# Hybrid decoder trunk on one core: activations and gated heads turned by VectorE and SBUF-to-SBUF transfers instead of TensorE

## The chip, the core and the metric

The kernel runs on one core of one Trainium2 chip. The metric is the device time of one execution in microseconds (us). The kernel before takes 2820.26 us, the median of three runs from 2818.15 to 2820.35 us.

A core has five instruction streams that the text calls by the profile's names: PE is TensorE (matrix products), DVE is VectorE, ACT is ScalarE, POOL is GpSimd, and SP is SyncE, which here does nothing but issue transfers. Each works through its own list in order. SBUF is the on-chip memory of 128 partitions; PSUM holds the products of PE.

## The reference, cut to what matters

The trunk has two layers, each a token mixer and a feed-forward network (FFN), over 256 tokens of width 2048 in float32.

```python
def swiglu(h, w_gate, w_up, w_down):            # D_FF = 5632
    return (jax.nn.silu(h @ w_gate) * (h @ w_up)) @ w_down

def gdn_mixer(h, w_in, conv_w, a_log, dt_bias, head_norm, w_out):   # layer 0, 32 value heads of 128
    ...
    o = gated_delta_rule_chunked(q, k, v, beta, g).astype(h.dtype)
    o = rmsnorm(o, head_norm) * jax.nn.silu(z.reshape(B, S, GDN_V_HEADS, GDN_HEAD_V))
    return o.reshape(B, S, GDN_VAL_DIM) @ w_out

def hgrn2_mixer(h, w_in, lower_bound, head_norm, w_out):            # layer 1, 16 heads of 128
    ...
    o = rmsnorm(o, head_norm) * jax.nn.silu(gate)
    return o.reshape(B, S, HGRN_VAL_DIM) @ w_out

for layer in range(DEPTH):
    h = h + mixer(rmsnorm(h, ...), ...)
    h = h + swiglu(rmsnorm(h, ffn_norm[layer]), ...)
return rmsnorm(h, final_norm)
```

Two products matter here: the one with `w_down`, whose left side is the gated activation, and the one with `w_out`, whose left side is the gated and normed head output. Both left sides are computed with tokens on the partitions, and PE needs them with features on the partitions. So they must be transposed, 256 tokens by some hundred features at a time.

## The kernel before, in words

**Stages.** In order of time: the GDN mixer (about 0 to 820 us), FFN 0 (to about 1550), the HGRN mixer (to about 2080), FFN 1 (to the end). Every stage is a list of *groups*. A group streams its weights from HBM in *halves* of 128 by 1024 floats (512 KB) and adds up its products in a PSUM tile `main`. Float32 products are made of three fast ones: each weight half `raw` is split into a rounded part `wh` (ACT) and the rest `wl` (DVE), each left side into `xt_h`/`xt_l`, `ht_h`/`ht_l` (`hth`, `htl` in the profile) or `ot_h`/`ot_l`, and PE multiplies high by high, high by low and low by high. A half in the FFN, or of a `w_out` product, is 12 PE products of 128 by 512.

**The weight stream.** `stream` issues one load of `raw` on SP for each half (945 in all) into four buffers, and `wh` and `wl` have four buffers each. A load waits until DVE has read the buffer it overwrites; `wh` waits until PE has used the one it overwrites.

**The order.** The program records all operations, and `plan` sorts them for each engine by an event-driven model: operations have costs (`price`, `COST`), transfers have an issue cost and a landing time, and the operation with the earliest due time goes first among those that are ready. The streamed `main` products keep their order on PE, and all other PE work ("aux") is fitted between them. What `plan` has settled is fixed; on the chip each engine only waits for what it needs.

**The work around the change.** `gate_up` in `ffn` ends a group of 8 halves with `h1` (128 tokens by two token halves by 256 features; `h` in the profile): ACT makes `sg`, DVE multiplies. Every second group, PE transposes the two `h1` tiles with eight 128x128 products by `ident` into two PSUM tiles, and ACT and DVE write `hth` and `htl` from there. There are 22 groups in each FFN, in two parts of 12 and 10, and after each part four `down` groups use `hth` and `htl`. `head_out` does the same for four heads at a time: `zs` (128 by 2 by 512) holds the gated heads, PE transposes it with eight products, and ACT and DVE write `ot_h` and `ot_l`. GDN calls it 8 times (head groups 0 to 7) and HGRN 4 times. `out_proj` then multiplies two head groups by a slice of `w_out`, in four groups of four halves; in each group the first two halves use the first head group, the last two the second.

`GDN_ORDER` sets the order of GDN's groups (k, v and z are the input products of a head group, o is an `out_proj` of two):

```python
GDN_ORDER = (
    "k0 k1 k2 k3 v0 v1 z0 z1 v2 z2 k4 k5 v3 z3 v4 k6 o0 k7 v5 z4 z5 o1 v6 v7 z6 z7 o2 o3"
)
```

So head group 7 is the last to be finished, while o2 streams, and o3 needs it in its third half. In `gdn_inverse`, four transfers on SP bring `wide` for a chain of small DVE operations.

Of the kernel before, what the change touches and what calls it, by code (L numbers as in the profile page):

```python
# [147 lines left out]
class Recorder:  # L148
# [158 lines left out]
    def plan(self):  # L307
# [70 lines left out]
        while len(order) < len(ops):  # L378
# [127 lines left out]
class Trunk:  # L506
# [116 lines left out]
    def mm_rows(self, ps, i, wh, wl, n_chunks, operand, halves=range(2)):  # L623

        for k in range(2):
            xh, xl = operand(2 * i + k)
            cols = slice(k * 512, (k + 1) * 512)
            for tt in halves:
                tok = slice(tt * P, (tt + 1) * P)
                out = ps[tt] if isinstance(ps, tuple) else ps[:, tt, :]  # L630
                for m, (s, w) in enumerate(((xh, wh), (xh, wl), (xl, wh))):
                    self.nc.tensor.matmul(
                        out, s[:, tok], w[:, cols],
                        start=(i == 0 and k == 0 and m == 0),
                        stop=(i == 2 * n_chunks - 1 and k == 1 and m == 2),
                    )
# [14 lines left out]
    def mm_cols(self, ps, i, wh, wl, n_k, n_f, n_chunks):  # L651

        for k in range(n_k):
            kt = i * n_k + k
            xh, xl = self.operand(kt)
            for f in range(n_f):
# [58 lines left out]
    def make_xt(self, cg, norm):  # L715
# [11 lines left out]
        for pair, ps in enumerate(two):  # L727
            for k in range(2):
# [36 lines left out]
    def ffn(self, j, after):  # L765
        nc, a = self.nc, self.a
        hts, h1s = {}, {}

        def gate_up(gi):
            def end(ps):  # L770
                h1 = self.tile(self.pool, [P, 2, T], "h1", bufs=4)
                for tt in range(2):
# [10 lines left out]
                pair = hts[gi // 2] = tuple(  # L783
                    self.tile(self.pool, [P, 4, T], f"ht{x}", F32R, bufs=max(FF_PARTS) // 2) for x in "hl"
                )
                two = self.aux(), self.aux()
                nc.together(*two)
                for of, tr in enumerate(two):
                    for k in range(2):
                        for tt in range(2):  # L790
# [4 lines left out]
                for of, tr in enumerate(two):  # L795
                    ht, lt = (t[:, 2 * of : 2 * of + 2, :].rearrange("p a t -> p (a t)") for t in pair)
                    nc.scalar.activation(ht, tr, AF.Copy)
                    nc.vector.tensor_tensor(out=lt, in0=tr, in1=ht.bitcast(F32), op=ALU.subtract)

# [377 lines left out]

    def head_out(self, o, zs, scale, norm):

# [31 lines left out]
        for tt in range(2):  # L1211
            for h in range(4):
# [4 lines left out]
                )  # L1217
        oh, ol = (t([P, 4, T], f"ot_{x}", dt=F32R, bufs=3) for x in "hl")
        two = self.aux(), self.aux()
        nc.together(*two)  # L1220
        for b, tr in enumerate(two):
            for h in range(2):
                for tt in range(2):
# [4 lines left out]
        for b, tr in enumerate(two):  # L1228
            s = slice(2 * b, 2 * b + 2)
            self.split_scaled(  # L1230
                oh[:, s, :].rearrange("p h t -> p (h t)"), ol[:, s, :].rearrange("p h t -> p (h t)"),
                tr, norm,
            )
        return oh, ol

    def gdn_o(self, hg, st):
# [85 lines left out]
    def out_proj(self, name, p, states, last, after):  # L1322
# [210 lines left out]
    def hgrn_o(self, g, st):  # L1533
# [4 lines left out]
        for tok in range(2):  # L1538
            for h in range(4):
# [201 lines left out]
```

## Time and profile before

| | |
|---|---|
| median of three runs | 2820.26 us |
| span of the profiled execution, first to last instruction | 2817.3 us |
| instructions | 39806 |
| PE busy | 2800.8 us, 15198 matmuls |
| DVE busy | 1744.5 us |
| ACT busy | 1423.1 us |
| POOL busy | 254.0 us |
| moved by the 16 DMA engines | 580.46 MB, 206 GB/s over the span |

The profile gives no separate time for the profiled execution; its span is 2817.3 us, and the median of the runs is 2.96 us above it.

How to read it: a row of operations gives line, engine, operation, output and inputs by the program's names, shapes, count, busy time and the mean duration of one in ns, then the idle time of its engine just before. All operations are issued by one helper, so every row has line 489, and tile names tell them apart. Matmul durations overlap: consecutive products start every 0.227 us although each lasts 0.39 us.

### The profile page before, as it was taken

The page shows a single profiled execution, that of the slowest core. Times are in us where ns is not written, and L with a number is a line of the kernel's source. Part 1 is how long each engine was busy: PE and PEld are TensorE (multiplying, and loading weights), DVE is VectorE, ACT ScalarE, POOL GpSimd, SP SyncE. Part 2 cuts the span into 40 slices and gives each one's busy share as a digit, 9 for nine tenths or more (in the row PEclk, how much of TensorE's full clock was granted, in tenths as well). Part 3 has the DMA queues.
Part 4 walks back from the last instruction along what each step waited for, and adds up shares of the span by engine and source line. Part 5 has one row for each costly group of instructions (what it writes and reads, how often), then busy time and mean ns, then how long its engine had stood idle before and what let it go on. Part 6 is the DMA issues. An engine that isn't in the chain of part 4 may idle for free.

```text
span 2817.3 us, 39806 instructions
## 1 busy us (share of the span) xinstructions
PE 2800.8 (99%) x15198; PEld 2392.1 (85%) x15198; DVE 1744.5 (62%) x2511; ACT 1423.1 (51%) x1988; POOL 254.0 (9%) x370
## 2 busy tenths in 40 slices
PE   9999999999999999999999999999999999999998
PEld 9988888888888888888888999999888888888887
DVE  6787888777765555445455677678555455445554
ACT  6646666564554444344445555556454444344443
POOL 1213222222110000000000100000110000000000
PEclk9999999999999999999999999999999999999999
DMA  7686668778786655666557645545785556765564
GB/s 254 197 275 206 211 221 260 219 216 263 228 252 193 188 193 187 223 223 189 192 189 227 203 149 164 168 149 163 228 265 189 192 188 207 224 204 193 187 199 160
DMA packets 162672, 580.46 MB, mean 206 GB/s; under 512 B 20138, under 2 KB 21306, under 8 KB 162352
## 3 DMA queue, kind: packets, MB, share of 16 engines
q1 hardware_dynamic: 138912, 503.15, 55.6%
q0 software_dynamic: 23280, 73.91, 8.5%
q8 instruction: 119, 1.95, 0.3%
q10 hardware_dynamic: 288, 0.85, 0.1%
q14 instruction: 73, 0.60, 0.1%
HBM read 550.52 MB, written 27.31 MB: 205 GB/s over the span
## 4 chain that ended last, share of the span: by engine, by line
PE 99%; ACT 0%; DVE 0%; issue 0%; POOLq 0%; POOL 0%; ACTq 0%
PE main L489 91%; PE aux L489 8%; ACT dec L489 0%; DVE wl L489 0%; ACT wh L489 0%; DVE u L489 0%; ACT xt_h L489 0%; DVE utmp L489 0%; DVE pre L489 0%; ACT y L489 0%; POOLq L1737 0%; ACT junk L489 0%; DVE xl L489 0%; DVE ot_l L489 0%; POOL coll L489 0%
## 5 line engine op out<-in xcount | busy, mean ns | idle before, releaser
L489 DVE TENSOR_TENSOR wl<-raw,wh 128x1024 fp32r<-128x1024 f32 x945 | 1161.5, 1230 | 974.7 <-ACT wh L489 972.1
L489 ACT ACTIVATE wh<-raw 128x1024 fp32r<-128x1024 f32 x945 | 1000.7, 1060 | 1270.9 <-PE main L489 1221.7
L489 PE MATMUL main<-wh,xt_h 128*128 128x512 f32 x2176 | 850.5, 391 | 0.6 <-ACT wh L489 0.6
L489 PE MATMUL main<-wh,xt_l 128*128 128x512 f32 x2176 | 849.9, 391 | 0.0
L489 PE MATMUL main<-wl,xt_h 128*128 128x512 f32 x2176 | 848.7, 390 | 0.9 <-DVE wl L489 0.9
L489 PEld LDWEIGHTS main<-wl,xt_h 128*128 128x128 f32 x2176 | 408.6, 188 | 84.7 <-DVE wl L489 1.3
L489 PEld LDWEIGHTS main<-wh,xt_h 128*128 128x128 f32 x2176 | 408.6, 188 | 84.0 <-ACT wh L489 1.0
L489 PEld LDWEIGHTS main<-wh,xt_l 128*128 128x128 f32 x2176 | 408.6, 188 | 83.7
L489 PE MATMUL main<-xt_h,wl 128*128 128x256 f32 (+1 forms) x1040 | 292.3, 281 | 1.5 <-DVE wl L489 1.5
L489 PE MATMUL main<-xt_l,wh 128*128 128x256 f32 (+1 forms) x1040 | 291.8, 281 | 0.3 <-DVE xt_l L489 0.3
L489 PE MATMUL main<-xt_h,wh 128*128 128x256 f32 (+1 forms) x1040 | 290.1, 279 | 0.0
L489 PE MATMUL main<-wh,hth 128*128 128x512 f32 x664 | 258.7, 390 | 0.0
L489 PE MATMUL main<-wh,htl 128*128 128x512 f32 x664 | 258.6, 389 | 0.0
L489 PE MATMUL main<-wl,hth 128*128 128x512 f32 x664 | 258.3, 389 | 0.0
L489 PEld LDWEIGHTS main<-xt_h,wh 128*128 128x128 f32 (+1 forms) x1040 | 195.6, 188 | 0.3
L489 PEld LDWEIGHTS main<-xt_h,wl 128*128 128x128 f32 (+1 forms) x1040 | 193.8, 186 | 2.0 <-DVE wl L489 1.9
L489 PEld LDWEIGHTS main<-xt_l,wh 128*128 128x128 f32 (+1 forms) x1040 | 193.8, 186 | 0.9 <-DVE xt_l L489 0.5
L489 PE MATMUL main<-wh,ot_l 128*128 128x512 f32 x384 | 151.2, 394 | 0.6 <-DVE ot_l L489 0.6
L489 PE MATMUL main<-wh,ot_h 128*128 128x512 f32 x384 | 150.6, 392 | 0.9 <-ACT ot_h L489 0.9
L489 PE MATMUL main<-wl,ot_h 128*128 128x512 f32 x384 | 150.3, 391 | 0.0
L489 PEld LDWEIGHTS main<-wh,htl 128*128 128x128 f32 x664 | 124.6, 188 | 25.9
L489 PEld LDWEIGHTS main<-wl,hth 128*128 128x128 f32 x664 | 124.6, 188 | 25.7
(207 smaller groups left out, 2226.5 us busy)
## 6 DMA issues: line engine op xcount, KB each, us to landing
raw<-in_ffn_gu SPq DMA_DIRECT2D x352, 512.0 KB, 3.8
raw<-in_ffn_d SPq DMA_DIRECT2D x176, 512.0 KB, 4.5
raw<-in_hgrn_in SPq DMA_DIRECT2D x128, 512.0 KB, 3.7
raw<-in_gdn_kq SPq DMA_DIRECT2D x64, 512.0 KB, 4.9
raw<-in_gdn_v SPq DMA_DIRECT2D x64, 512.0 KB, 4.6
raw<-in_gdn_z SPq DMA_DIRECT2D x64, 512.0 KB, 4.9
raw<-in_gdn_out SPq DMA_DIRECT2D x64, 512.0 KB, 4.9
x_home<-x POOLq DMA_DIRECT2D x36, 512.0 KB, 5.1
```

Of the source, the lines that this page charges most:

```text
L489: getattr(getattr(tc.nc, op.eng), op.method)(*args, **kw)
```

## The change

Both transposes leave PE. A new function `turn` has DVE turn each 32 by 32 block of the tile in place of its position (one instruction), and then sixteen transfers on SP move the blocks, one for each pair of a source quarter and a target quarter of the partitions, back into the tile that was turned. Each transfer moves 32 partitions by 128 floats (16 KB) for `h1`, or by 256 floats (32 KB) for `zs`. After them the columns are in an order that the rearranged views undo. `h1` is turned after every group and no longer in pairs. ACT and DVE write the high and low parts from SBUF and no longer from PSUM; `ot_l` takes four DVE instructions of 128 by 256 in place of two of 128 by 512. The tiles that hold the parts are laid out by token half first, so `mm_rows` takes its left side by token half. Where `zs` is turned, the blocks go through the buffer of `r` (GDN) or `v` (HGRN), which is no longer needed then. In `plan`, SP is taken to be busy for 0.1 us instead of 0.45 with a transfer smaller than a fifth of a weight half. The transposes of the residual stream (`make_xt`) stay on PE.

```diff
-            clock[e] = at + max(0.45, LOAD_EVERY * op.share) if e == "sync" else done
+            clock[e] = at + max(0.1 if op.share < 0.2 else 0.45, LOAD_EVERY * op.share) if e == "sync" else done
...
+    def turn(self, x, blocks):
+        nc = self.nc
+        width = x.shape[1] // 4
+        nc.vector.transpose(
+            blocks.rearrange("p (c a j) -> p a c j", c=4, j=32), x.rearrange("p (a c i) -> p a c i", c=4, i=32)
+        )
+        for q in range(4):
+            for c in range(4):
+                nc.sync.dma_start(
+                    x[32 * c : 32 * c + 32, q * width : (q + 1) * width],
+                    blocks[32 * q : 32 * q + 32, c * width : (c + 1) * width],
+                )
+        return x.rearrange("p (q a j) -> p a q j", q=4, j=32)
...
     def ffn(self, j, after):
-                h1s[gi] = h1
-                if gi % 2 == 0:
-                    return
-                two = self.aux(), self.aux()
...
-                            nc.tensor.transpose(
-                                tr[:, k * T + tt * P : k * T + (tt + 1) * P],
-                                h1s[gi - 1 + of][:, tt, k * P : (k + 1) * P], self.ident,
-                            )
...
+                blocks = self.tile(self.pool, [P, 512], "blocks", bufs=2)
+                turned = self.turn(h1.rearrange("p t c -> p (t c)"), blocks)
...
+                nc.scalar.activation(as_turned(ht), turned, AF.Copy)
+                nc.vector.tensor_tensor(
+                    out=as_turned(lt), in0=turned, in1=as_turned(ht.bitcast(F32)), op=ALU.subtract
+                )
...
-    def head_out(self, o, zs, scale, norm):
+    def head_out(self, o, zs, scale, norm, blocks):
...
-                    nc.tensor.transpose(
-                        tr[:, h * T + tt * P : h * T + (tt + 1) * P],
-                        zs[:, tt, (2 * b + h) * P : (2 * b + h + 1) * P], self.ident,
-                    )
...
+        turned = self.turn(zs.rearrange("p t c -> p (t c)"), blocks)
+        nc.scalar.activation(as_turned(oh), turned, AF.Copy, scale=norm)
+        for q in range(4):
+            nc.vector.scalar_tensor_tensor(
+                out=as_turned(ol)[:, :, q], in0=turned[:, :, q], scalar=norm,
+                in1=as_turned(oh.bitcast(F32))[:, :, q], op0=ALU.mult, op1=ALU.subtract,
+            )
```

How the planned order moves is shown at four places.

ACT in an FFN, before: one pair of groups, from `sg` of the second group.

```order
L489 ACTIVATE sg_9108<-main_8948,rstd_61 128x256
L489 ACTIVATE sg_9114<-main_8948,rstd_61 128x256
L489 ACTIVATE wh_9122<-raw_9065 128x1024
L489 ACTIVATE wh_9143<-raw_9083 128x1024
L489 ACTIVATE hth_8761<-aux_9140 128x512
L489 ACTIVATE hth_8761<-aux_9149 128x512
L489 ACTIVATE wh_9175<-raw_9102 128x1024
```

ACT in an FFN, now, from `sg` of any group:

```order
L489 ACTIVATE sg_9889<-main_9706,rstd_61 128x256
L489 ACTIVATE sg_9895<-main_9706,rstd_61 128x256
L489 ACTIVATE wh_9904<-raw_9846 128x1024
L489 ACTIVATE wh_9934<-raw_9864 128x1024
L489 ACTIVATE wh_9959<-raw_9883 128x1024
L489 ACTIVATE wh_9977<-raw_9907 128x1024
L489 ACTIVATE hth_8839<-h_1476_9902 128x512
L489 ACTIVATE wh_9997<-raw_9943 128x1024
```

`hth` comes after the fourth `wh` behind `sg` and no longer after the second, once for every group, and reads the turned `h1` instead of a PSUM tile.

SP at the same place, now, with the waits of each transfer (DVE, and DMAHW0 to DMAHW7, the eight completion counters that SP's transfers take in turn); before, the weight loads stand alone there:

```order
L489 DMA raw_9907<-in_ffn_gu 128x1024 [waits DMAHW5_49,DMAHW1_49,DVE_49]
L489 DMA h_1476_9902<-blocks_9914 32x128 [waits DMAHW6_49,DVE_49]
L489 DMA h_1476_9902<-blocks_9914 32x128 x3
L489 DMA h_1476_9902<-blocks_9914 32x128 [waits DMAHW2_49]
...
L489 DMA h_1476_9902<-blocks_9914 32x128 [waits DMAHW2_49]
L489 DMA raw_9943<-in_ffn_gu 128x1024 [waits DMAHW3_49,DVE_49]
L489 DMA h_1476_9902<-blocks_9914 32x128 [waits DMAHW4_49]
L489 DMA h_1476_9902<-blocks_9914 32x128 [waits DMAHW5_49]
L489 DMA h_1476_9902<-blocks_9914 32x128 [waits DMAHW6_49]
L489 DMA raw_9962<-in_ffn_gu 128x1024 [waits DMAHW7_49,DVE_49]
```

Thirteen transfers of a turn, one weight load, three transfers, the next load. A transfer takes a counter again only when the transfer eight places earlier has landed, so at most eight are under way.

On SP in the middle of GDN two turns have the four `wide` transfers of the next head group's chain close behind them, now:

```order
L489 DMA zs_6339<-r_4588 32x256 x13
L489 DMA raw_6684<-in_gdn_out 128x1024
L489 DMA zs_6339<-r_4588 32x256 x3
L489 DMA wide_6705<-n_dram_6556 32x1024 x4
...
L489 DMA zs_6454<-r_5935 32x256 x2
L489 DMA raw_7331<-in_gdn_z 128x1024
L489 DMA wide_7343<-n_dram_7184 32x1024 x4
```

Before, only weight loads stood ahead of `wide`. A third turn, that of head group 0, stands three loads ahead of a `wide`.

PE at the end of GDN, before: the first group of o3, where it passes from head group 6 (`ot_h_8056`) to head group 7 (`ot_h_8418`).

```order
L489 MATMUL main_8360<-wh_8326,ot_h_8056 128x512
L489 MATMUL main_8360<-wl_8334,ot_h_8056 128x512
L489 MATMUL main_8360<-wh_8326,ot_l_8070 128x512
L489 MATMUL aux_8410<-head_58,zs_7913 128x128 x4
L489 MATMUL aux_8415<-head_58,zs_7913 128x128 x4
L489 MATMUL main_8360<-wh_8341,ot_h_8418 128x512
L489 MATMUL main_8360<-wl_8356,ot_h_8418 128x512
L489 MATMUL main_8360<-wh_8341,ot_l_8429 128x512
```

PE there now, and then DVE there now (`r_7531` is the buffer of the blocks):

```order
L489 MATMUL main_8417<-wh_8386,ot_h_8218 128x512
L489 MATMUL main_8417<-wl_8400,ot_h_8218 128x512
L489 MATMUL main_8417<-wh_8386,ot_l_8228 128x512
L489 MATMUL main_8417<-wh_8397,ot_h_8489 128x512
L489 MATMUL main_8417<-wl_8409,ot_h_8489 128x512
L489 MATMUL main_8417<-wh_8397,ot_l_8492 128x512
```

```order
L489 SCALAR_TENSOR_TENSOR zs_7961<-aux_8351,ocol_8394,zs_7961 128x128 x4
L489 TENSOR_TENSOR wl_8446<-raw_8327,wh_8419 128x1024
L489 STREAM_TRANSPOSE r_7531<-zs_7961 128x8x4x32
L489 TENSOR_TENSOR x_8266<-x_8266,main_8306 128x1024
L489 TENSOR_TENSOR wl_8474<-raw_8353,wh_8443 128x1024
L489 TENSOR_TENSOR wl_8483<-raw_8412,wh_8462 128x1024
L489 SCALAR_TENSOR_TENSOR ot_l_8492<-zs_7961,gdn_hn_356,ot_h_8489 128x8x32 x4
```

The eight transposes are gone from PE and nothing takes their place: the product with `ot_h` of head group 7 follows directly. On DVE the turn stands behind one `wl`, and `ot_l` two `wl` further on. On SP the sixteen transfers of this turn stand together, with no weight load between them.

More of the change, by code (lines that the diff above doesn't have):

```diff
@@ L632, in mm_rows @@
                     self.nc.tensor.matmul(
-                        out, s[:, tok], w[:, cols],
+                        out, s[:, tt, :], w[:, cols],
                         start=(i == 0 and k == 0 and m == 0),
@@ L654, in mm_cols @@
             kt = i * n_k + k
-            xh, xl = self.operand(kt)
+            xh, xl = (x.rearrange("p t j -> p (t j)") for x in self.operand(kt))
             for f in range(n_f):
@@ L667, in mm_gates @@
         for kt in range(16):
-            xh, xl = self.operand(kt)
+            xh, xl = (x.rearrange("p t j -> p (t j)") for x in self.operand(kt))
             at = slice(kt * 64, (kt + 1) * 64)
@@ L675, in operand @@
     def operand(self, kt):
-        return self.xt_h[kt // 4][:, kt % 4, :], self.xt_l[kt // 4][:, kt % 4, :]
+        return tuple(x[kt // 4][:, kt % 4, :].rearrange("p (t j) -> p t j", t=2) for x in (self.xt_h, self.xt_l))
     def sumsq(self, cg):
@@ L779, in end @@
                     )
[L780 to L798 removed]
+                blocks = self.tile(self.pool, [P, 512], "blocks", bufs=2)
+                turned = self.turn(h1.rearrange("p t c -> p (t c)"), blocks)
+                hts[gi] = ht, lt = tuple(
+                    self.tile(self.pool, [P, 2, 2, P], f"ht{x}", F32R, bufs=max(FF_PARTS)) for x in "hl"
+                )
+                as_turned = lambda x: x.rearrange("p t n (q j) -> p (t n) q j", q=4)
+                nc.scalar.activation(as_turned(ht), turned, AF.Copy)
+                nc.vector.tensor_tensor(
+                    out=as_turned(lt), in0=turned, in1=as_turned(ht.bitcast(F32)), op=ALU.subtract
+                )
             gu = a[f"ffn_gu{j}"]
@@ L806, in down @@
         def down(part, cg):
-            first = sum(FF_PARTS[:part]) // 2
+            first = sum(FF_PARTS[:part])
             n = FF_PARTS[part] // 2
@@ L811, in operand @@
             def operand(kt):
-                h, l = hts[first + kt // 4]
-                return h[:, kt % 4, :], l[:, kt % 4, :]
+                h, l = hts[first + kt // 2]
+                return h[:, :, kt % 2, :], l[:, :, kt % 2, :]
             last = part == len(FF_PARTS) - 1
@@ L1217, in head_out @@
                 )
[L1218 to L1223, printed above, removed]
-                    nc.tensor.transpose(
-                        tr[:, h * T + tt * P : h * T + (tt + 1) * P],
-                        zs[:, tt, (2 * b + h) * P : (2 * b + h + 1) * P], self.ident,
-                    )
[L1228 to L1232, printed above, removed]
+        oh, ol = (t([P, 2, 4, P], f"ot_{x}", dt=F32R, bufs=3) for x in "hl")
+        turned = self.turn(zs.rearrange("p t c -> p (t c)"), blocks)
+        as_turned = lambda x: x.rearrange("p t n (q j) -> p (t n) q j", q=4)
+        nc.scalar.activation(as_turned(oh), turned, AF.Copy, scale=norm)
[3 more added lines that the diff above has]
+                in1=as_turned(oh.bitcast(F32))[:, :, q], op0=ALU.mult, op1=ALU.subtract,
             )
@@ L1273, in gdn_o @@
         )
-        st["ot"] = self.head_out(o, st["zs"], scale, self.gdn_hn)
+        st["ot"] = self.head_out(
+            o, st["zs"], scale, self.gdn_hn, r.rearrange("p t h d -> p (t h d)")
+        )
     def gdn(self, after):
@@ L1546, in hgrn_o @@
                 )
-        st["ot"] = self.head_out(o, st["zs"], 0.5, self.hgrn_hn)
+        st["ot"] = self.head_out(
+            o, st["zs"], 0.5, self.hgrn_hn, v.rearrange("p t c -> p (t c)")
+        )
     def hgrn(self, after):
```

5 lines of the change are left out of this document (2 added, 3 removed).

## The prediction, made before the changed kernel ran

> **What bounds the kernel now.** I read the page first (engines, clock, chain), then who PE waits for, then the chain in order of time at the transposes.
>
> ```profile
> PE 2800.8 (99%) x15198; PEld 2392.1 (85%) x15198; DVE 1744.5 (62%) x2511; ACT 1423.1 (51%) x1988; POOL 254.0 (9%) x370
> PEclk9999999999999999999999999999999999999999
> PE 99%; ACT 0%; DVE 0%; issue 0%; POOLq 0%; POOL 0%; ACTq 0%
> ACT wh L489 <- PE main L489: 1221.7, 821, 7.8
> SPq L489 <- DVE wl L489: 1916.3, 769, 12.8
> ```
>
> PE is the bound everywhere: 99% of the chain that ended last is PE, at full granted clock. ACT waits 1221.7 us for PE to give back `wh` buffers, so the weights run ahead of PE by all four buffers. Whatever PE no longer does is therefore gained, as long as nothing else comes so late that PE has to wait.
>
> **What the transposes cost on PE.** The chain shows it directly:
>
> ```profile
> 973.49 0.87 PE aux L489 x8
> 974.36 43.54 PE main L489 x192
> 1017.90 0.87 PE aux L489 x8
> 1999.27 0.87 PE aux L489 x8
> L489 PE MATMUL aux<-head,h 128*128 128x128 f32 x176 | 22.8, 272 | 0.0
> L489 PE MATMUL aux<-head,zs 128*128 128x128 f32 x96 | 12.8, 274 | 0.0
> ```
>
> In FFN 0 two groups of products take 43.54 us (192 at 0.227 us, 2.72 us for a half of 12), and eight transposes 0.87 us between them; eight in HGRN take the same. There are 176 + 96 = 272 transposes, 34 batches of eight: 34 x 0.87 = 29.6 us. Of these 19.1 lie in the FFNs (22 batches), 7.0 in GDN (8), 3.5 in HGRN (4). This is the gain if the new path stays hidden.
>
> **What the new path costs.** One turn is an instruction on DVE, sixteen issues on SP, their landing, then ACT and DVE.
>
> ```profile
> L489 DVE STREAM_TRANSPOSE inv<-u 32x256 f32<-32x256 f32 x32 | 13.8, 432 | 1.7 <-ACT u L489 1.0
> L489 DVE TENSOR_TENSOR htl<-aux,hth 128x512 fp32r<-128x512 f32 x44 | 28.2, 682 | 0.0
> L489 DVE SCALAR_TENSOR_TENSOR acc<-pre,conv,acc 128x256 f32<-128x256 f32 x96 | 43.0, 479 | 0.1
> L489 DVE SCALAR_TENSOR_TENSOR ot_l<-aux,gdn_hn,ot_h 128x512 fp32r<-128x512 f32 x16 | 11.5, 743 | 1.5 <-ACT ot_h L489 1.5
> L489 DVE TENSOR_TENSOR wl<-raw,wh 128x1024 fp32r<-128x1024 f32 x945 | 1161.5, 1230 | 974.7 <-ACT wh L489 972.1
> L489 ACT ACTIVATE hth<-aux 128x512 fp32r<-128x512 f32 x44 | 23.5, 587 | 0.0
> 111.38 1.73 SPq L489 DMA_DIRECT2D wide<-n_dram  x4
> raw<-in_ffn_gu SPq DMA_DIRECT2D x352, 512.0 KB, 3.8
> n_dram<-nmat POOLq DMA_DIRECT2D x64, 16.0 KB, 3.9
> DMA to landing us min/median/max: 1.8/4.3/8.1
> q0 software_dynamic: 250, 0.14, 8.0%
> ```
>
> The transposing instruction exists: 256 elements in 432 ns, as fast as other DVE work of that length, so 512 should take what `htl` does, 0.68 us, and 1024 what `wl` does, 1.2 us. DVE gains 44 x 0.68 = 30 us in the FFNs, and 12 x (1.2 + 4 x 0.448 - 2 x 0.74) = 18 us in the mixers: 0.448 is one of `acc`, which has the length of the new `ot_l` (43.0 / 96), and 0.74 one `ot_l` now. DVE had 38% of the span idle, so this costs nothing by itself. ACT's work stays the same: one `hth` of 512 for each group as now.
>
> SP's price for an issue is read from four back-to-back small ones, 1.73 / 4 = 0.43 us; sixteen are 6.9 us. The landing of an SBUF-to-SBUF transfer is not in this trace. The bounds are the shortest and the longest of the rows that touch `n_dram`, 1.8 and 8.1 us; I take 3.8 in the FFNs and 3.9 in GDN, since a small transfer that queues behind a load on the same engines should land about when the load does, and the one 16 KB transfer that starts in SBUF takes 3.9. The engines themselves are no limit: the last row is POOL's queue over 98 to 105 us, 250 small packets (0.56 KB each) in 8.0% of 16 x 7 us, 36 ns a packet; a turn's 512 packets are 18 us over 16 engines, 1.2 us each, once in 21.8 us.
>
> Since at most eight of SP's transfers are under way, the ninth waits for the first. So the last lands, with landing time L, after max(3.4, L) + 7 or 8 issues x 0.43 + L.
>
> **In the FFNs.** The place is the end of a group:
>
> ```profile
> 881.49 0.87 DVE L489 SCALAR_TENSOR_TENSOR h<-main,rstd,sg 128x256 f32<-128x256 f32 x2
> 881.98 1.06 ACT L489 ACTIVATE wh<-raw 128x1024 fp32r<-128x1024 f32 x1 [0.93 <-PE main L489]
> 884.70 1.06 ACT L489 ACTIVATE wh<-raw 128x1024 fp32r<-128x1024 f32 x1 [1.66 <-PE main L489]
> 883.07 1.23 DVE L489 TENSOR_TENSOR wl<-raw,wh 128x1024 fp32r<-128x1024 f32 x1 [0.71 <-ACT wh L489]
> ```
>
> `h` is ready at 882.4, turned at 883.1. The ninth transfer goes at 886.9 (L = 3.8), the sixteenth, with one load between, at 890.3, and lands at 894.1. ACT has `hth` behind the fourth `wh`, the one that starts at 881.98 + 3 x 2.72 = 890.1, so ACT stands for 3 us, ends `hth` at 894.7 and the fifth `wh` at 895.8; `wl` follows at 897.0. PE needs that half only at 901.0: the fifth `wh` may start at 892.9, when PE has used the first half, and PE then has three halves (8.2 us) in hand. So 4.0 us remain and PE waits for nothing. What is queued behind the turn on SP: one load is due at 884.4, when `wl` has freed its buffer, and goes at 889.1; it lands at about 892.9, before the fifth `wh` can start at 894.7. The next goes 2 to 3 us late and is covered in the same way. Eight loads and sixteen small issues are 10.3 us of SP in every 21.8, so it catches up. `down` needs the last `hth` eleven halves (30 us) after its group, against some 15 for the new path. FFN gain: 19.1, cover 4.0 us.
>
> **In HGRN** the rows of the last head group are these:
>
> ```profile
> L489 DVE SCALAR_TENSOR_TENSOR zs<-aux,ocol,zs x8: 342/343/346, 1992.9 to 1996.2; 128x128 f32<-128x128 f32 x8
> L489 ACT ACTIVATE zs<-main,rstdh x2: 671/674/677, 1988.9 to 1989.5; 128x512 f32<-128x512 f32 x2
> ```
>
> `zs` is done at 1996.5 (its last instruction starts at 1996.2); turned at 1997.8, landed at 1997.8 + 10.8, split 2.9 us later, 2011.5. Its user comes 16 halves of o-groups and two more after the gate's group, which ended by 1989: at 2038. Gain kept: 3.5.
>
> **At the end of GDN** there is no cover:
>
> ```profile
> 786.87 2.15 DVE L489 SCALAR_TENSOR_TENSOR zs<-aux,ocol,zs 128x128 f32<-128x128 f32 x8
> 790.98 1.03 PE L489 MATMUL aux<-head,zs 128*128 128x128 f32 x8
> 792.86 0.50 PE L489 MATMUL main<-wh,ot_h 128*128 128x512 f32 x1 [0.85 <-ACT ot_h L489]
> 794.20 0.50 PE L489 MATMUL main<-wh,ot_l 128*128 128x512 f32 x1 [0.61 <-DVE ot_l L489]
> ```
>
> PE already waits for head group 7 here, first for `ot_h`, then `ot_l`. With the change: `zs` done at 789.0, one `wl` (1.2), turned at 791.4; the ninth transfer 3.9 later, the sixteenth 3.0 after that, landed at 802.2; `ot_h` (1024 elements, 1.06 like a `wh`) at 803.3; four `ot_l` at 0.448 each, 805.1. The product that started at 794.20 starts 10.9 later. The planned order has three more products between the chain's last aux work and this point (28 and 24 against 25 and 24, 0.7 us), and the 0.87 us of this batch were counted above as gained, so the loss is 10.9 - 0.7 + 0.9 = 11.1 us. By the bounds of L (1.8 and 8.1) it is 8.5 and 19.5; 11.1 is taken, by the row of the same size that starts in SBUF.
>
> **In the middle of GDN** seven turns stand among chains that are tight:
>
> ```profile
> 240.00:440.00 200.00, 197.98 (x1463) 174.69 (x1464) 170.31 (x370) 128.51 (x239) 61.63 (x87) 1.00 0.71 221
> 120.86 0.18 DVE L489 TENSOR_TENSOR utmp<-u,wide 128x31 f32<-128x31 f32 x1
> DMA to landing us min/median/max: 4.7/5.0/5.1
> PE main L489 <- DVE wl L489: 2.0, 2, 1.1
> PE main L489 <- ACT wh L489: 0.6, 1, 0.6
> ```
>
> DVE (third number) is busy for 170 of 200 us. The plan takes a turn for 16 x 0.1 = 1.6 us of SP, the chip takes 6.9: what stands behind it comes 5.3 us late. Three of the seven have `wide` close behind. Its last transfer, issued at 112.7, lands at 117.8 and is used at 120.86: 3.1 us of cover, so 2.2 us of each delay reach the chain and PE, which holds that chain's products in its list. That is 6.6 us. Bounds: nothing, if later slack takes it up, and 7 x 5.3 = 37 us, if each turn's whole delay reaches PE. I take 6.6, since the other four have only loads behind them, which are covered as in the FFNs.
>
> **The sum.** -29.6 + 11.1 + 6.6 = -11.9 us. The profiled 2817.3 become 2805.4; the median stands 2.96 above that span, so 2820.26 - 11.9 = 2808.4.
>
> **The rivals.** (1) *SP starves the FFNs (slower).* The cover of 4.0 us ends where 2L + 3.4 (eight issues) + 2.9 (`hth`, `wh`, `wl`) = 17.9 us, from 883.1 to 901.0: at L = 5.8. The rows for both sides:
>
> ```profile
> wide<-n_dram SPq DMA_DIRECT2D x4, 128.0 KB, 6.2
> 850.00:1150.00 300.00, 300.00 (x1349) 248.93 (x1349) 150.61 (x146) 129.57 (x145) 1.46 (x2) 1.00 0.61 194
> ```
>
> At the 6.2 us that `wide` took at 179 us, beside a load, PE waits 0.8 us in each of 44 turns, 35 us in all, near 2843; at 7 us it is 2.4 each, near 2914. For it: sixteen transfers follow each other, more than any row has. Against: loads of 512 KB land in 3.8 us in the FFNs, and the engines are busy for 61% there (the number before the last). Chance 0.10. In a harsher form the landings do not overlap: sixteen of the shortest are 29 us, longer than a group of 21.8, and each of 44 turns costs 7 us and the loads' own issues (3.4 us) besides, some 460 us. Against this, four `wide` issued within 1.73 us all landed 4.7 to 5.1 us after their issue. Chance 0.02. The Trainium skill, "DMA: Bandwidth & Descriptors", section "Rules for kernel authors", points to this form: it advises to join many small transfers into one, as those under 64 KB are mostly overhead. By that rule a turn would pay sixteen overheads; the trace's `wide` rows do not agree that they add up.
>
> (2) *GDN eats everything.* If all seven turns pass on their 5.3 us: -29.6 + 11.1 + 37 = +18.5, 2839; between, 2816 to 2839. For it DVE's 85%, against it that PE waits only for `wh` and `wl` in GDN before its end. Chance 0.16. (3) *GDN gives back little:* tail 8.5, middle nothing: -21, 2799; down to 2793 if the chain gets ahead of the plan by the time PE saves. Chance 0.17. That the transposes do not go is excluded by the order. My own case keeps 0.55.
>
> **How the numbers follow.** The likeliest gives 2808, with 2800 to 2816 as its own range. From the cases: 2793 to 2832 leaves out (1) and the far end of (2). A measurement tells 0.2%, 5.6 us, from no change. Faster: 0.53 of my case and (3), 0.70. Same: 0.02 and half of (2), 0.10. Slower: the rest, 0.20.
>
> **What would show it.** PE loses 272 matmuls, and between FFN groups the chain has no gap, 87 us for four of them. A PE wait of about 10 us for `ot_h` and `ot_l` stands near 790 us. SP's small issues are 0.43 us apart. ACT stands 3 us before each `hth` without PE waiting. I am wrong if PE waits for `wh` or `wl` in the FFNs, if a small transfer lands after 6 us or more, or if GDN's end moves by more than 25 us.

## The result, and the profile after

The changed kernel takes 2858.14 us (median of four runs, 2856.97 to 2859.84) against 2819.49 us for the kernel before in the same comparison: ratio 1.0137, 95% interval 1.0123 to 1.0151. It is 38.7 us slower, where 11.9 us less was forecast, and lies outside the predicted range (2793 to 2832). The profiled execution spans 2855.3 us (before: 2817.3).

First the engines, the chain's shares by engine, and the waits (us in total, times, longest) of the changed kernel:

```profile
PE 2795.0 (98%) x14926; PEld 2375.2 (83%) x14926; DVE 1784.7 (63%) x2591; ACT 1417.2 (50%) x1976; POOL 257.1 (9%) x370
PE 51%; DMA 11%; SPq 11%; DVE 3%; issue 2%; ACT 2%; ACTq 0%; POOLq 0%; POOL 0%; DVEq 0%
ACT wh L489 <- PE main L489: 690.8, 470, 7.8
DVE htl L489 <- ACT hth L489: 261.4, 43, 7.7
ACT hth L489 <- DMA h<-blocks: 259.7, 39, 8.2
ACT wh L489 <- DMA raw<-in_ffn_gu: 132.3, 175, 2.9
PE main L489 <- ACT ot_h L489: 11.6, 1, 11.6
PE main L489 <- ACT r L489: 5.1, 1, 5.1
```

PE lost its 272 transposes, and yet PE's share of the chain fell from 99% to 51%: transfers and SP's queue now share in setting the end. ACT waits for PE (the sign that the weights run ahead) for 691 us instead of 1222, and for loads in the FFNs 175 times.

Next, where in time. Each stage ends with sixteen `xt_l` of the next stage's input; the last start of these, before (three rows) and after (three rows):

```profile
L489 DVE SCALAR_TENSOR_TENSOR xt_l<-aux,head,xt_h x16: 473/476/478, 804.5 to 841.0; 128x256 fp32r<-128x256 f32 x16
L489 DVE SCALAR_TENSOR_TENSOR xt_l<-aux,head,xt_h x16: 473/476/478, 1487.0 to 1572.5; 128x256 fp32r<-128x256 f32 x16
L489 DVE SCALAR_TENSOR_TENSOR xt_l<-aux,head,xt_h x16: 472/476/479, 2048.2 to 2084.7; 128x256 fp32r<-128x256 f32 x16
...
L489 DVE SCALAR_TENSOR_TENSOR xt_l<-aux,head,xt_h x16: 473/474/478, 851.6 to 888.1; 128x256 fp32r<-128x256 f32 x16
L489 DVE SCALAR_TENSOR_TENSOR xt_l<-aux,head,xt_h x16: 473/476/479, 1529.1 to 1613.0; 128x256 fp32r<-128x256 f32 x16
L489 DVE SCALAR_TENSOR_TENSOR xt_l<-aux,head,xt_h x16: 473/476/479, 2086.5 to 2122.4; 128x256 fp32r<-128x256 f32 x16
```

By differences, GDN takes 47.1 us more (forecast +10.7), FFN 0 6.6 less (forecast -9.6), HGRN 2.8 less (-3.5), FFN 1 0.3 more (-9.6).

**GDN: a turn in the queue.** SP and ACT of the changed kernel around 265 us, then windows (start and end; length; busy time of PE, of PE's weight loads, DVE, ACT and POOL; granted clock; DMA share; GB/s):

```profile
257.05 10.11 SPq L489 DMA_DIRECT2D zs<-r  x16
267.26 1.77 SPq L489 DMA_DIRECT2D raw<-in_gdn_kq  x3
269.34 4.61 SPq L489 DMA_DIRECT2D wide<-n_dram  x4
...
264.10 1.06 ACT L489 ACTIVATE wh<-raw 128x1024 fp32r<-128x1024 f32 x1
268.56 1.26 ACT L489 ACTIVATE r<-main,rstd 128x512 f32<-128x512 f32 x2 [3.40 <-DMA zs<-r]
269.71 1.15 ACT L489 ACTIVATE ot_h<-zs,gdn_hn 128x1024 fp32r<-128x1024 f32 x1
...
262.00:264.00 2.00, 2.00 (x23) 1.17 (x21) 0.88 (x1) 0.70 (x2) 0.30 (x1) 1.00 0.18 49
264.00:270.00 6.00, 0.91 (x18) 0.77 (x17) 1.23 (x1) 2.56 (x5) 0.00 (x0) 0.71 0.39 119
270.00:272.00 2.00, 2.00 (x10) 2.00 (x11) 1.11 (x3) 1.50 (x3) 0.75 (x1) 0.50 0.74 201
274.00:276.00 2.00, 2.00 (x20) 2.00 (x19) 0.45 (x1) 1.51 (x2) 0.00 (x0) 1.00 0.98 322
```

Sixteen issues hold SP for 10.1 us, 0.63 each. `r` has two buffers, and one of them now holds the turned blocks: ACT cannot copy the next v group from `main` until the transfers have read it, and PE, which needs `main` back, stands for 5.1 us. Then the clock column: PE runs at 0.50 until about 273, ten products in 2 us, where there are twenty at 1.00. The stop costs twice.

**The tail**, where 11.1 us were forecast:

```profile
824.83 10.33 SPq L489 DMA_DIRECT2D zs<-r  x16
836.67 1.15 ACT L489 ACTIVATE ot_h<-zs,gdn_hn 128x1024 fp32r<-128x1024 f32 x1 [9.33 <-DMA zs<-r]
837.87 0.79 PE L489 MATMUL main<-wh,ot_h 128*128 128x512 f32 x1 [11.62 <-ACT ot_h L489]
```

The number is about right by luck, as two errors largely offset each other: the sixteen issues took 10.3 us where 6.9 were forecast, and the transfers landed after 2.5 us (median of `zs<-r`) where 3.9 were taken. From the first issue to `ot_h` it was 11.8 us, 10.8 by the forecast.

**The FFNs: a bundle in front of the loads.** SP's row, then ACT's, of one group in FFN 0:

```profile
1062.70 9.10 SPq L489 DMA_DIRECT2D h<-blocks  x13
1071.90 0.53 SPq L489 DMA_DIRECT2D raw<-in_ffn_gu  x1
1072.47 1.77 SPq L489 DMA_DIRECT2D h<-blocks  x3
1074.34 9.68 SPq L489 DMA_DIRECT2D raw<-in_ffn_gu  x7
...
1068.21 1.06 ACT L489 ACTIVATE wh<-raw 128x1024 fp32r<-128x1024 f32 x1 [0.24 <-DMA raw<-in_ffn_gu]
1076.45 0.63 ACT L489 ACTIVATE hth<-h 128x512 fp32r<-128x512 f32 x1 [7.17 <-DMA h<-blocks]
1078.82 1.06 ACT L489 ACTIVATE wh<-raw 128x1024 fp32r<-128x1024 f32 x1 [0.79 <-DMA raw<-in_ffn_gu]
```

For 11.5 us SP issues one load, while PE uses up four halves. ACT stands 7 us before `hth` (3 were forecast) and then waits for loads.

### The profile page after: what moved, and what is told of

It reads as the page before. It is cut to its first block, busy times and chain, and to the rows that moved or that the text cites. A ratio compares the mean times of both kernels' runs of the same rounds, so it can differ in the third digit from the quotient of the medians.

```text
span 2855.3 us, 40750 instructions
## 1 busy us (share of the span) xinstructions
PE 2795.0 (98%) x14926; PEld 2375.2 (83%) x14926; DVE 1784.7 (63%) x2591; ACT 1417.2 (50%) x1976; POOL 257.1 (9%) x370
## 4 chain that ended last, share of the span: by engine, by line
PE 51%; DMA 11%; SPq 11%; DVE 3%; issue 2%; ACT 2%; ACTq 0%; POOLq 0%; POOL 0%; DVEq 0%
PE main L489 47%; SPq L489 11%; DMA raw<-in_ffn_gu 9%; PE aux L489 5%; ACT wh L489 2%; DVE wl L489 2%; DMA raw<-in_ffn_d 1%; DMA h<-blocks 0%; DVE h L489 0%; DMA zs<-r 0%; DVE blocks L489 0%; DMA raw<-in_hgrn_in 0%; DMA raw<-in_gdn_out 0%; DVE r L489 0%; DMA raw<-in_hgrn_out 0%
## 5 line engine op out<-in xcount | busy, mean ns | idle before, releaser
L489 DVE TENSOR_TENSOR htl<-h,hth 128x512 fp32r<-128x512 f32 x44 | 30.5, 693 | 267.4 <-ACT hth L489 261.4
L489 ACT ACTIVATE hth<-h 128x512 fp32r<-128x512 f32 x44 | 27.8, 632 | 293.5 <-DMA h<-blocks 259.7
L489 PE MATMUL main<-wh,ot_h 128*128 128x512 f32 x384 | 152.8, 398 | 12.5 <-ACT ot_h L489 11.6
```

Of the source, the lines that this page charges most:

```text
L489: getattr(getattr(tc.nc, op.eng), op.method)(*args, **kw)
```

## The experiments

All runs but e12 edit the changed kernel. "GDN" and so on are differences to the kernel before by the `xt_l` rows of the one profiled execution; "us" is the median of all executions, and ratios are to the kernel before, with their 95% interval. In e4, e6 and e15 the profiled execution was some 4, 11 and 5 us above the median, so their stage columns are on the high side. e10 and e14 are given in the text.

| run | us | ratio | GDN | FFN 0 | HGRN | FFN 1 |
|---|---|---|---|---|---|---|
| changed kernel | 2858.1 | 1.0137 (1.0123, 1.0151) | +47.1 | -6.6 | -2.8 | +0.3 |
| e1 turns in the FFNs alone | 2821.2 | 1.0004 (0.9995, 1.0013) | +1.5 | -1.8 | +0.1 | +2.3 |
| e2 turns in the mixers alone | 2863.4 | 1.0155 (1.0141, 1.0169) | +48.8 | 0.0 | -3.0 | 0.0 |
| e3 no transfers | 2795.2 | 0.9911 (0.9896, 0.9926) | -1.2 | -9.8 | -3.5 | -9.3 |
| e4 five transfers by DRAM | 2822.6 | 1.0008 (0.9999, 1.0017) | +30.7 | -9.8 | -3.5 | -9.9 |
| e5 price 0.63 in the plan | 2821.1 | 1.0001 (0.9992, 1.0011) | +26.6 | -9.8 | -3.5 | -9.8 |
| e6 other buffers for the blocks | 2874.9 | 1.0201 (1.0178, 1.0224) | +69.5 | -1.2 | -2.7 | +1.4 |
| e7 transfers issued by POOL | 2824.3 | 1.0013 (1.0004, 1.0023) | +18.8 | -5.6 | -3.5 | -5.3 |
| e8 e4 with GDN on PE | 2797.2 | 0.9918 (0.9904, 0.9933) | +1.3 | -9.8 | -3.5 | -9.8 |
| e9 e5 with GDN on PE | 2797.0 | 0.9918 (0.9902, 0.9935) | +1.6 | -9.8 | -3.4 | -9.9 |
| e11 e5, head group 7 on PE | 2807.7 | 0.9958 (0.9944, 0.9973) | +12.9 | -9.8 | -3.4 | -9.9 |
| e13 bundles kept, `hth` later | 2826.8 | 1.0023 (1.0013, 1.0034) | +1.3 | +5.3 | -1.2 | +2.2 |
| e15 e11 with e6's buffers | 2807.0 | 0.9955 (0.9940, 0.9970) | +15.9 | -9.8 | -3.5 | -9.6 |

**e1 and e2, one part at a time.** In e1 `head_out` keeps the eight transposes, in e2 `gate_up` does:

```diff
 # e1, head_out
-        turned = self.turn(zs.rearrange("p t c -> p (t c)"), blocks)
...
+                    nc.tensor.transpose(tr[...], zs[:, tt, (2 * b + h) * P : (2 * b + h + 1) * P], self.ident)
...
 # e2, gate_up
-                turned = self.turn(h1.rearrange("p t c -> p (t c)"), blocks)
...
+                            nc.tensor.transpose(tr[...], h1s[gi - 1 + of][:, tt, k * P : (k + 1) * P], self.ident)
...
```

> Turns in the two FFNs alone; GDN and HGRN keep TensorE's transposes. By the stage times of the changed kernel (FFN 0 -6.7, FFN 1 +0.3), if the stages add up: 2819.5 - 6.4 = 2813 us. By the prediction's own term for the FFNs (22 batches x 0.87, all hidden): 2800. If what the FFNs lost came from a plan upset elsewhere and not from the turns beside the loads, they are worth the full 19 here as well.

> Turns in GDN and HGRN alone; the FFNs keep TensorE's transposes. If the loss is GDN's own (47.2 us there, HGRN -2.8): 2864 us, slower than the whole change. By the prediction's terms (-10.5 + 11.1 + 6.6): 2827. The gated heads' chain is then to show the same stops of PE at the turns (5.1, 3.2, 1.8, 3.6, 4.4, 4.8, 11.6 us) and the granted clock below 1 behind those of about 2 us and more.

e2 is as expected: the loss is GDN's. e1 came out 8 us above the first of its numbers: alone, the FFNs' turns gain nothing at all, 2821.17 against 2820.03, so what they lose is not lost by GDN's turns. (GDN's +1.3 to +1.6 in e1, e8, e9 and e13, which leave it on PE, was not looked into; in e10 and e14, which leave it there too, it is -0.7 and -0.2.)

**e3, no transfers.**

```diff
-        for q in range(4):
-            for c in range(4):
-                nc.sync.dma_start(x[...], blocks[...])
-        return x.rearrange("p (q a j) -> p a q j", q=4, j=32)
+        return blocks.rearrange("p (q a j) -> p a q j", q=4, j=32)
```

> The sixteen transfers of each turn are left out: ACT and DVE read the tile that VectorE's 32x32 turn has written, so that the blocks stand in the wrong order in the operands and the output is not the reference's. Everything else of the change stays. Theory A (SP's issues, 16 x 0.63 us, and what they hold up): nearly the whole 29.6 us come, with the tail at GDN's end back to about 1 us: 2790 to 2795, and no clock below 1. Rival B (VectorE's turn, the four ot_l for two, operands read from SBUF: engine work, not transfers): within 10 us of the changed kernel, 2848 to 2858.

The kernel leaves out the transfers, so its output is not the reference's. Theory A's number, 2795.2, though the granted clock did fall below 1 in GDN, near 236 and 267 us. VectorE's turn, the four `ot_l` and the operands from SBUF cost the FFNs and HGRN nothing. In GDN 1.2 of the 7.0 us are gained: what is left of the change without transfers eats some 6 there.

**e4, one transfer to DRAM and four back.**

```diff
-        for q in range(4):
-            for c in range(4):
-                nc.sync.dma_start(x[...], blocks[...])
+        kept = self.tile(self.dram, [P, 4 * width], f"kept{width}", bufs=2)
+        nc.sync.dma_start(kept, blocks)
+        for c in range(4):
+            nc.sync.dma_start(
+                x[32 * c : 32 * c + 32, :].rearrange("p (q w) -> p q w", q=4),
+                kept[:, c * width : (c + 1) * width].rearrange("(q p) w -> p q w", q=4),
+            )
```

> One transfer to DRAM and four back instead of sixteen in SBUF: 5 issues for 16, the same bytes twice, two landings one behind the other. Theory A (the number of issues on SP): a turn holds SP for 3 us instead of 10, the FFNs gain 15 to 19 us, GDN's stops shrink: 2805 to 2825. Rival (the way itself, from turned blocks to landed operand, is what costs): two landings of 2 to 4 us are about as long as sixteen issues and one landing (12.6 us), so GDN keeps its loss: 2845 or more.

The FFNs got all of their gain back, GDN kept 30.7 us, so both halves of the expectation hold in one stage each. But fewer issues is not the only way, as the next run shows.

**e5, the price in the plan.** One number; every instruction and byte stays.

```diff
-            clock[e] = at + max(0.1 if op.share < 0.2 else 0.45, LOAD_EVERY * op.share) ...
+            clock[e] = at + max(0.63 if op.share < 0.2 else 0.45, LOAD_EVERY * op.share) ...
```

> The planner's price of a turn's issue is set from 0.1 to the 0.63 us that the chip takes; instructions, bytes and buffers stay, only the order that the plan writes for the engines changes. Theory P (the plan, which believes a turn's way to take 6.4 us where the chip takes 12.6, sets ACT and DVE to wait where other work was ready): GDN loses 25 of its 47 us, the FFNs put hth later and gain some: 2815 to 2835. Theory A (SP's own time is the loss, whatever the order): 16 issues still hold SP for 10 us, so 2850 to 2860.

37 us come back from the order alone. SP and ACT of an FFN 0 group in this run:

```profile
1044.22 0.33 SPq L489 DMA_DIRECT2D raw<-in_ffn_gu  x1
1044.60 1.84 SPq L489 DMA_DIRECT2D h<-blocks  x2
1046.94 0.33 SPq L489 DMA_DIRECT2D raw<-in_ffn_gu  x1
1047.32 1.77 SPq L489 DMA_DIRECT2D h<-blocks  x3
...
1063.63 1.06 ACT L489 ACTIVATE wh<-raw 128x1024 fp32r<-128x1024 f32 x1 [1.66 <-PE main L489]
1064.60 0.61 ACT L489 ACTIVATE hth<-h 128x512 fp32r<-128x512 f32 x1
```

Mostly two or three transfers now go between two loads, over the whole group; `hth` comes a group later and without a wait, and the `wh` ahead of it waits for PE and not for a load. In the FFNs the same sixteen issues hide entirely.

**e13, which way the bundle hurt.** GDN on PE, price 0.1 as in the change, and 8.5 us more landing time in the plan for a turn's transfers: SP keeps 13 and 3 in a row, but `hth` and `htl` stand later on ACT and DVE.

```diff
+            if op.eng == "sync" and op.share < 0.1:
+                op.lag += 8.5
```

> GDN on TensorE, sixteen transfers, price 0.1 as in the change, but the planner is told that a turn's transfer lands 8.5 us later (the 16 x 0.53 us that its price leaves out). SP's order keeps its bundles of 13 and 3; only hth and htl stand later on ACT and DVE. If ACT's standing before hth is the way by which the FFNs lost: FFN 0 and 1 near 722 and 723 us, 2797. If the loads held behind the bundle are: they stay near 730 and 735, 2815.

ACT no longer stands before `hth`, and it helps nothing: 2826.8, FFN 0 even 5 us over before. The wait has moved to the loads (381 us, 132 in the changed kernel; the helper's line is 491 in this run):

```profile
ACT wh L491 <- DMA raw<-in_ffn_gu: 381.4, 167, 8.9
1065.68 8.60 SPq L491 DMA_DIRECT2D h<-blocks  x13
```

So ACT's stand before `hth` is not needed for the loss: the loads held behind the bundle make it by themselves. How much ACT's stand adds in the changed kernel, where FFN 0 still gains 6.6 us, is not shown.

**e10 and e14, twice the issues.** GDN on PE; each transfer is cut in two (32 a turn, the same bytes), booked at 0.63 (e10) and 0.3 us (e14).

```diff
+                for s in range(2):
...
-                    x[32 * c : 32 * c + 32, q * width : (q + 1) * width],
...
+                    x[32 * c : 32 * c + 32, q * width + s * half : q * width + (s + 1) * half],
...
```

> The same with every transfer cut in two, 32 issues a turn, the same bytes. By the issue time alone SP then needs 8 x 0.37 + 32 x 0.63 = 23.1 us for a group that PE does in 21.8, so the FFNs' groups become SP's: 44 x 1.3 = 57 us less what the down products (11 loads and no turn in 30 us) let it catch up: 2815 to 2860. If transfers are not what SP's time limits (landing or bytes): 2797.

> 32 half transfers a turn again, but booked at 0.3 us each (what sixteen at 0.6 are), so that the plan weaves four or five of them between two loads as it does with two or three. SP needs 23.1 us for a group of 21.8. If SP's time is a limit by itself: 22 x 1.3 = 29 us for each FFN, less some 10 that the down products give back: FFNs near 740, 2825 to 2850. If the time was all the plan's: 2797 to 2802.

Both are far above their expectations: e10 3154.8 us (ratio 1.1190; 1.1173, 1.1207), e14 2959.2 (1.0492; 1.0474, 1.0509). In e10 the plan itself books 32 x 0.63 and 8 loads of 1.3 for a group of 21.8 us, so it puts turns off until PE waits for them: 274 us for `hth`, in 20 stops. e14 has no such backlog in its plan and shows SP's own limit. A full round of its weave runs from 1060.84 to 1086.27 us, 25.4 us for 32 transfers and 8 loads, mainly because a load behind small transfers takes SP 0.53 us (one of these 1.30) and not 0.33:

```profile
1060.84 3.04 SPq L489 DMA_DIRECT2D h<-blocks  x5
1068.21 0.53 SPq L489 DMA_DIRECT2D raw<-in_ffn_gu  x1
1086.27 3.04 SPq L489 DMA_DIRECT2D h<-blocks  x5
```

3.6 us over the group's 21.8, 22 times, is 79; FFN 0 took 804.3 us, 82.6 more than the 721.7 with sixteen. In PE's windows 49.5 us of FFN 0 are idle time and 18.9 us slow clock. SP's time is a limit by itself, but sixteen issues are well below it: 25.4 less 16 x 0.63 leaves 15.3 us of 21.8.

**e6 and e15, the reuse of `r`.** GDN's blocks go to two buffers of tag `w` instead of `r`, by two turns of 512 elements; e6 under the price of 0.1, e15 under 0.63 with head group 7 on PE.

```diff
-            o, st["zs"], scale, self.gdn_hn, r.rearrange("p t h d -> p (t h d)")
+            o, st["zs"], scale, self.gdn_hn,
+            *(self.tile(self.pool, [P, 512], "w", bufs=2) for _ in range(2)),
...
```

> In GDN the turned blocks go to two buffers of tag w (dead by then) instead of r, by two turns of 512 elements instead of one of 1024; r is free as soon as its products are done. Theory C (ACT's copy of the next v group has to wait until the transfers have read r, and PE behind it): the stop of 5.1 us at 265 shrinks to the 1.3 us that it is without transfers, so do the two like it, with their slow clock: GDN loses 8 to 15 us less, 2843 to 2850. Rival (the landing and SP's issues hold the chain anyway): within 4 us of 2858.

> Price 0.63, head group 7 on TensorE as in the run before, and GDN's blocks in two buffers of tag w instead of r. If the reuse of r makes the stop of 5.0 us near 270: it goes, with its 2.6 us of slow clock, 2800 to 2803. If a buffer of w is late in its place, or the transfers are waited for anyway: 2806 to 2815.

In both the stop near 265 for `r` is gone, and neither is faster: e6 is slower than both its numbers, and e15 lies where its second case put it. In e6 stops for ACT's `w` of 4.6 and 6.6 us stand at 285 and 460, and the tail grew from 11.6 to 20.5 us. In e15 PE stops 4.8 us at 800 for `zs` (the transposes of head group 7) and 2.1 us for `w` at 477. The reuse makes that stop, but not the loss: the next late thing takes its place.

**e7, POOL issues the transfers.**

```diff
-                nc.sync.dma_start(
+                nc.gpsimd.dma_start(
```

> The sixteen transfers of a turn are issued by POOL, which is busy for 9%, instead of SP. POOL's small issues take 0.56 to 0.59 us, so the way from turn to landing is as long as before, but the weights' queue is free. Theory A (the loads that stand behind the issues on SP): the FFNs get their 19 us back (FFN 0 near 722, FFN 1 near 723 us), HGRN stays. In GDN POOL is part of the chain (pow, n_dram, u_dram): 10 us there for each turn; GDN is to stay 30 to 60 us longer. Sum 2825 to 2860. If the FFNs' loss is the length of the way (rival), they stay at 725 and 733.

At 2824.3 it ends 0.7 us below the range. GDN at +18.8 is the best of all runs that turn every head group and move the blocks, below the expected 30 to 60, and the FFNs get 5.6 and 5.3 us, not 19 together. Why POOL's transfers do not hide in the FFNs was not followed up.

**e11, the tail alone.** `head_out` transposes on PE where `blocks` is `None`:

```diff
-            o, st["zs"], scale, self.gdn_hn, r.rearrange("p t h d -> p (t h d)")
+            o, st["zs"], scale, self.gdn_hn, None if hg == 7 else r.rearrange("p t h d -> p (t h d)")
```

> Price 0.63, all turns as in the change, but head group 7 of GDN by TensorE's transposes. The tail (9.3 us stop for ot_h and 2.9 us of slow clock after it, in the run with the price alone) goes back to before's 1.5 us: 2821 - 10 = 2811, GDN's end near 857. If the tail only shows what the middle has already lost, GDN's end stays near 867.

GDN's end moves by 13.7 us, to 853.9: the tail adds to the rest and does not stand in for it.

**e8 and e9, the gain without the loss.** GDN keeps PE's transposes, FFNs and HGRN turn by DRAM (e8), or with the change's own sixteen transfers and the price of 0.63 (e9).

```diff
-            o, st["zs"], scale, self.gdn_hn, r.rearrange("p t h d -> p (t h d)")
+            o, st["zs"], scale, self.gdn_hn, None
```

> The FFNs and HGRN turn by one transfer to DRAM and four back, GDN keeps TensorE's transposes. If the stages add up as measured (-9.8, -9.9, -3.5, GDN 0): 2820.0 - 23.2 = 2797, faster than both kernels. If the gain in the FFNs hung on a plan that GDN's turns had set, less: 2800 to 2815.

> As the run with transfers through DRAM and GDN on TensorE, but with the change's own sixteen SBUF-to-SBUF transfers and the planner's price of 0.63 us. Theory P (the sixteen issues fit between the loads once the plan knows their price): 2796 to 2799, the same as with five. Theory A (fewer issues are needed): 2805 or more.

Both came out as expected, 2797.16 and 2797.02: faster than both kernels by 0.8% and 2.1%. The 23 us are the price of 22 + 4 batches of 0.87, all of it.

**e12, stops and issues by themselves.** Not the kernel, and one execution only:

```python
for r in range(5):
    for ns in ((128,), (512,), (1024,), (1024, 256), ...):        # nine lengths
        for i in range(50 + 3 * r):
            nc.tensor.matmul(ps[:, 0:512], lhs, rhs, start=True, stop=True)
        nc.scalar.activation(stop[:, 0:128], ps[:, 0:128], AF.Copy)
        ...                                                       # copies of ns elements
        nc.scalar.activation(lhs, stop[:, 0:128], AF.Copy)
```

> Not the kernel: PE runs streams of 50 to 62 products of 128x512 and between them waits for ACT copies, by design for some 0.9, 1.4, 2, 2.5, 3, 3, 4, 5 and 7.5 us, five times each; afterwards SP issues rows of sixteen transfers of several shapes. Clock: in the changed kernel single stops of 1.3 us and more were followed by 3.4 us or twice that at half clock. If length decides, each stop above some 1.5 us costs 1.7 us of slow products behind it, none below 1 us does; if a window that runs by itself decides, stops of one length sometimes cost and sometimes don't. Issue price: theory S (a source in SBUF makes it 0.59) gives 0.59 for every SBUF-to-SBUF form and 0.33 to 0.43 for those that read DRAM; theory R (32 rows in 16 small pieces, whatever the source) gives 0.59 for 32 rows from DRAM also and less for 128 rows.

At full clock a stream takes 0.2265 us a product and some 0.31 us besides. Beyond that, the streams behind stops of 0.77 and 1.43 us lost nothing (10 of 10); behind 1.86 us one of five lost 1.6 us; behind 2.3, 2.5 and 2.95 us four, three and two of five lost 1.5 to 1.7; behind 4.0 us and more each (14 of 14) lost 1.3 to 2.9. Six us after a stop of 1.43, twice after one of 1.86 and once after one of 4.0 (windows as above, granted clock third from the end):

```profile
324.30:330.30 6.00, 6.00 (x27) 4.96 (x28) 0.00 (x0) 0.00 (x0) 0.00 (x0) 1.00 0.00 0
339.10:345.10 6.00, 6.00 (x26) 4.99 (x27) 0.00 (x0) 0.00 (x0) 0.00 (x0) 1.00 0.01 3
498.30:504.30 6.00, 6.00 (x19) 4.74 (x20) 0.00 (x0) 0.00 (x0) 0.00 (x0) 0.72 0.01 3
407.80:413.80 6.00, 6.00 (x14) 4.73 (x15) 0.00 (x0) 0.00 (x0) 0.00 (x0) 0.50 0.00 0
```

The same length costs or does not: the second of the expected rules. In the kernel shorter stops were enough: half clock stands behind one of 1.3 us (e3, near 267 us), and behind two of 0.8 and 0.9 us that start 1.4 us apart (e3 and e5, near 236 us). So the 1.43 us that cost nothing here, behind streams of dense products, are no bound for the kernel. The issues on SP, ns each (shortest/median/longest), by where the ends lie (`near` and `far` in SBUF, `kept` in DRAM, `in_x` the input):

```profile
L60 SPq DMA_DIRECT2D near<-far x16: 588/589/752, 2.3 to 12.0; - x16
L60 SPq DMA_DIRECT2D near<-kept x16: 414/419/1225, 22.8 to 30.7; - x16
L60 SPq DMA_DIRECT2D kept<-far x16: 347/419/421, 31.2 to 38.1; - x16
L60 SPq DMA_DIRECT2D near<-far x16: 469/599/602, 38.6 to 48.4; - x16
L60 SPq DMA_DIRECT2D big<-in_x x4: 327/330/339, 57.6 to 64.2; - x4
```

32 rows of 128 floats, SBUF to SBUF: 0.589. 32 rows from or to DRAM: 0.419. 128 rows from DRAM (`big<-kept`): median 0.430. 128 rows, SBUF to SBUF: 0.599. A 512 KB load: 0.330. So neither theory as put: it takes both ends in SBUF, whatever the number of rows.

## Why the prediction was wrong, point by point

**The price of an issue: mis-sized.** The prediction took 0.43 us from `wide`, the nearest row. `wide` reads DRAM, and e12 gives 0.42 for that; a turn's transfer has both ends in SBUF and takes 0.59, 0.63 from one to the next. Sixteen are 10.1 us, not 6.9. It had no bound: both ends of the range were put on the landing, which came out shorter (median 2.5 us) than the 3.8 assumed, and the threshold of rival 1 (L at 5.8) was one on the wrong number. The `wide` rows, by which the harsher form of rival 1 was held small, are of 128 KB each and could not show what sixteen transfers of 16 KB cost; the changed kernel shows that SP pays for sixteen issues one after another, while the landings overlap.

```profile
h<-blocks SPq DMA_DIRECT2D x704, 16.0 KB, 2.5
L489 SPq DMA_DIRECT2D h<-blocks x704: 507/588/1861, 908.6 to 2752.5; - x176
```

**"In the FFNs ... PE waits for nothing": failed.** The cover of 4.0 us had to hold 3.2 us more of issues, and the loads behind them cost 0.53. Of the 19.1 us, 6.3 came in the whole change and none in e1. "What is queued behind the turn on SP" was asked and answered for one load; e13 shows that the row of loads behind the bundle is enough for it. PE's own rows have 6.4 us of waits in the FFNs, 6.2 of them for `wl`, about half of the 13.3 us that the FFNs lose against e5; no row shows the rest.

**The middle of GDN, 6.6 us: failed, by far the largest.** GDN changed by +47.1. Adding the 7.0 that the transposes saved and taking off the tail (11.62 + 0.49 against 0.85 + 0.61 before, 10.7, and 2.5 of slow clock behind it) leaves 40.9 us, above even the upper bound of 37. That bound counted each turn's delay once. It left out what ACT and DVE, which work in order, hold back while they wait for a landing, the reuse of `r`, and the clock. The account closes, though. PE's idle time in a stage is the window less its busy time; before and after:

```profile
0.00:841.00 841.00, 834.45 (x5347) 720.97 (x5348) 648.87 (x1333) 511.09 (x907) 200.09 (x304) 1.00 0.74 234
0.00:889.00 889.00, 845.60 (x5286) 727.24 (x5287) 655.27 (x1358) 510.03 (x900) 200.44 (x303) 0.97 0.70 226
```

Idle 6.6 and 43.4 us. What the slow clock costs is the sum, over windows of 1 us, of PE's busy time by one less the granted clock:

| run | idle over before's 6.6 | slow clock | batches gone | sum | measured |
|---|---|---|---|---|---|
| changed kernel | 36.8 | 16.1 | -7.0 | 45.9 | 47.1 |
| e3 no transfers | 3.3 | 3.4 | -7.0 | -0.3 | -1.2 |
| e4 by DRAM | 22.3 | 15.5 | -7.0 | 30.8 | 30.7 |
| e5 price 0.63 | 22.5 | 10.7 | -7.0 | 26.2 | 26.6 |
| e7 POOL | 19.1 | 5.6 | -7.0 | 17.7 | 18.8 |
| e11 head group 7 on PE | 12.7 | 5.6 | -6.1 | 12.2 | 12.9 |

Of idle time and slow clock together, the clock is a quarter to two fifths, but for e3 where both are small. The Trainium skill, "TensorE: Matmul & The Clock Gate", section "What's actually happening", describes the half-rate state and a free-running window of about 3.4 us; an estimate from that page is 1.7 us for one window at half rate, and the steps of 1.5 to 1.7 us behind stops of 1.86 to 2.95 us in e12 agree; those behind longer stops, 1.3 to 2.9 us, are not all one such window. Its section "HAM oscillation — how this bites in real kernels" puts the rule as no idle gaps over some 3.4 us; here the trace does not agree, since a stop of 1.86 us was enough in one case of five and one of 2.3 us in four of five.

**What the plan believes.** The prediction saw that the plan takes a turn for 1.6 us of SP, and drew on it only in GDN, as a delay of what stands behind. e5 shows its real size: 37 us, the whole difference between a loss and none, is the order that this one number writes. The change itself had lowered it from 0.45; no run turns with the 0.45.

**Right:** 0.87 us a batch and their sum (FFNs and HGRN give 23.1 in e9, 22.6 forecast), the tail (10.7 idle for 11.1, by the offsetting errors above, and with 2.5 us of slow clock that was not forecast), DVE's times (turns 0.71 and 1.24, forecast 0.68 and 1.2; `ot_l` 0.48 for 0.45), HGRN, and that the sixteen landings overlap. Rival 2 named the right stage, rival 1 the right queue; each was held too small, and both came at once.

**Open:** the 12.9 us that GDN still loses in e11. e15 moved a stop and gained nothing, and e3, without transfers, gains 1 of 7 us, so these chains have no room for a longer way; which of their links sets it was not settled.

## What to carry to other kernels

Moving work off the bounding engine gains what it cost there only if the new way's length and its queue have room. Take the issue price from a row with the same ends (SBUF to SBUF is not DRAM to SBUF), put it into whatever sets the order before judging the idea, and weave small transfers between the loads rather than in a row ahead of them. In a stage of tight chains a stop of PE is not paid by its length alone: count the slow clock behind it, and leave work there on the engine that does it at once.

## What the runs showed of the hardware that was not expected

An SBUF-to-SBUF transfer takes SP 0.59 us to issue, 32 or 128 rows alike, against 0.42 for 32 rows with one end in DRAM (0.43 for 128 rows from there), and 0.33 for a 512 KB load; a load right behind such transfers takes 0.53. PE stops of 1.86 to 2.95 us were followed by half clock in ten cases of twenty, stops of 1.43 us or less in none of ten, and stops of 4 us or more in all fourteen; those are stops between dense streams (e12), and in the kernel one of 1.3 us (e3) and a close pair of 0.8 and 0.9 us (e3, e5) were followed by it too.
